# Activation halves as one 512-column matmul, and second products by pairs of output tiles, in a two-block transformer kernel

## The chip, the cores and the metric

The kernel runs on one core of a Trainium2 chip. The metric is the device time of one execution in microseconds (us). The core's engines run in parallel and wait for one another by semaphores: TensorE (PE, with its weight loads shown apart as PEld), VectorE (DVE), ScalarE (ACT), GpSimd (POOL), and SyncE (SP), which issues most transfers.

## What is computed

Two transformer blocks in float32 on one sequence of 256 rows and 1024 channels. The first block has two layers; the second has one, with a modulation by a condition vector c:

```python
for i in range(2):                                   # first block, F = 2816
    x = x + 0.5 * swiglu_ffn(rms_norm(x, ffn1_norm[i]), ffn1_w_in[i], ffn1_w_out[i])
    h = rms_norm(x, mix_norm[i])
    x = x + (pool_mixer(h, ...) if i == 0 else nsa_mixer(h, ...))
    x = x + memory_cross_attention(rms_norm(x, xattn_norm[i]), rms_norm(mem, mem_norm[i]), ...)
    x = x + 0.5 * swiglu_ffn(rms_norm(x, ffn2_norm[i]), ffn2_w_in[i], ffn2_w_out[i])
x = rms_norm(x, final_norm)
# second block: shift, scale, gate = parts of silu(c) @ ada_w + ada_b
u = rmsnorm(x, norm_mix) * (1 + scale1) + shift1
...                                                  # u @ w_in: three attentions, and gates
x = x + gate1 * ((gates[0] * y_a + gates[1] * y_b + gates[2] * y_c) @ w_o)
u2 = rmsnorm(x, norm_mlp) * (1 + scale2) + shift2
x = x + gate2 * (jnp.square(jax.nn.relu(u2 @ w_ff1)) @ w_ff2)     # 4096 hidden
return rmsnorm(x, norm_final)

def swiglu_ffn(h, w_in, w_out):
    g, u = jnp.split(h @ w_in, 2, axis=-1)
    return (jax.nn.silu(g) * u) @ w_out
```

## The kernel before

Activations live transposed: channels on the 128 partitions, the 256 rows on the free axis, eight tiles of channels. Every float32 operand is split exactly into two float32r parts, hi and lo. A product of a 128x128 weight tile with 256 columns is three float32r matmuls of 256 columns that add up in PSUM (`mm3`, L154 to L159): w_hi with x_hi (L157), w_hi with x_lo (L158), w_lo with x_hi (L159). Each loads its own weights. Where the result has rows on partitions (`row_tiles`), the activations are the loaded side and 256 columns of a weight slab move.

Weights come in slabs of 1 MB, [128, 2048] a partition, by transfers that SP issues into four `raw` buffers. Each slab is split in halves of 1024 elements: ACT casts the hi part (`hi`, L98), DVE subtracts it from the raw weights for the lo part (`lo`, L104), into six buffers for each part.

A swiglu feed-forward (`_swiglu`) runs over 11 slabs j, each of two hidden tiles. One slab takes two `w_in` slabs (gate and up halves) and one `w_out` slab. `product` makes 32 products for the two hidden tiles, gate and up beside each other in one PSUM bank for each tile. `evacuate` (L397 to L407) multiplies a bank by the rows' norm factor (DVE, 128x512, L399), takes the silu (ACT, L401), the product of the halves (DVE, L403), and splits the result (ACT L98, DVE L104). `output(j - 2)` makes the 16 second products of a slab two slabs later; they add up in four PSUM banks `acc`, which are held through the whole feed-forward. `residual` (L463 to L471) adds the result to x at the end, by eight DVE instructions of 128x256.

Other work is traced between the slabs. `middle[j]` is a step of it at slab j. The `modulation` steps (L1025 to L1030) are DVE work on slabs of ada_w, on 9 of 11 slabs in the second feed-forward of layer 0 and in the first of layer 1, and on 6 in the last one. `fill` traces steps of a generator that waits for gaps; `mem_kv`, the memory's keys and values for the cross-attention, is one with 8 slabs a layer, and `fill(after)` places some of its steps at the ends of phases. In `_xattn` each head's products with `w_o` are part of that head's stage of the pipeline (L697 to L704). `merge` and `_mlp` are built like the feed-forward, with slabs of w_o, of w_ff1 and w_ff2.

The order on each engine is the order in which the program is traced, as far as the tile scheduler leaves it; it moves instructions of different phases past each other where their operands allow it. PSUM has eight banks of [128, 512] float32: four in the pool `pm` (products on their way out), and four that a phase takes for its own.

## Time and profile before

| what | value |
|---|---|
| runs | 1582.41, 1581.73 us and one of 6651.41; median 1582.41 us |
| the profiled execution's own span | 1590.3 us |
| PE busy | 1558.1 us, 12979 matmuls |
| DVE busy | 1120.5 us |
| ACT busy | 831.0 us |
| POOL busy | 115.4 us |
| read from HBM | 289.42 MB, 183 GB/s over the span |

The profile is of one execution, seen by the hardware's profiler. It gives each engine's busy time, and for each idle stretch what ended it. Busy shares are means over stages of different kinds: a share of a stage says more than one of the span. PE's matmuls overlap in the pipeline, so the duration shown of one matmul is longer than the distance between the starts of two; distances, or a count over a stretch without gaps, give the rate. The granted clock is PE's, as a share of its full one.

### The profile page before, as it was taken

Reading aid. Unit: us, or ns where it says so; the run is one execution under the profiler, and the core shown is the slowest. Engines: PE = TensorE matmul, PEld = TensorE weight load, DVE = VectorE, ACT = ScalarE, POOL = GpSimd, SP = SyncE. Lnnn points to the kernel's source line nnn. Section 1 sums busy time; section 2 is a strip of 40 time slices with the busy share of each in tenths; the row PEclk is TensorE's granted clock in tenths of the full one; section 3 lists DMA queues with packets and bytes.
Section 4 is the critical chain, followed back from the end, with each engine's and each line's share of the span. In section 5 each row is a group of like instructions: output and inputs, shape, how many; then the busy total and the mean of one; then the engine's idle time right before and its main releaser. Section 6 shows DMA issues by size and latency. Waiting matters only on the chain.

```text
span 1590.3 us, 31387 instructions
## 1 busy us (share of the span) xinstructions
PE 1558.1 (98%) x12979; PEld 1523.9 (96%) x12979; DVE 1120.5 (70%) x2034; ACT 831.0 (52%) x1401; POOL 115.4 (7%) x195
## 2 busy tenths in 40 slices
PE   8999999999999999999999998999999999999998
PEld 8999999999999999999986997999999999999998
DVE  6676589688787688885677666887587755885553
ACT  6544457554445444453467554444453786464443
POOL 3010022030001100011000213000000000000000
PEclk9999999999999999999999999999999999999999
DMA  8645655457776677766741335686644644545540
GB/s 267 232 167 177 206 172 168 132 182 248 248 246 214 214 241 248 254 212 195 212 107 54 132 108 164 212 266 226 202 140 127 189 138 155 184 159 188 186 160 27
DMA packets 232364, 292.52 MB, mean 184 GB/s; under 512 B 7805, under 2 KB 210460, under 8 KB 232220
## 3 DMA queue, kind: packets, MB, share of 16 engines
q1 hardware_dynamic: 231756, 289.84, 56.2%
q8 instruction: 102, 1.67, 0.4%
q10 hardware_dynamic: 464, 0.66, 0.1%
q14 instruction: 42, 0.34, 0.1%
HBM read 289.42 MB, written 1.07 MB: 183 GB/s over the span
## 4 chain that ended last, share of the span: by engine, by line
PE 89%; DVE 4%; ACT 3%; POOL 2%; issue 1%; DMA 1%; DVEq 0%; ACTq 0%; POOLq 0%
PE ps L157 28%; PE ps L158 27%; PE ps L159 27%; DVE wl L104 1%; ACT wh L98 1%; PE tr L1392 1%; PE ps L874 1%; PE o L935 1%; PE ps L483 1%; ACT pn L957 0%; DVE isc L1477 0%; DVE iwk L1485 0%; DMA dl<-in_diff_lambda_dram 0%; POOL s L339 0%; PE ps L358 0%
## 5 line engine op out<-in xcount | busy, mean ns | idle before, releaser
L98 ACT CAST wh<-raw 128x1024 fp32r<-128x1024 f32 (+1 forms) x500 | 506.7, 1028 | 569.3 <-PE ps L158 459.2
L104 DVE TENSOR_TENSOR wl<-raw,wh 128x1024 fp32r<-128x1024 f32 (+1 forms) x500 | 605.9, 1225 | 256.9 <-ACT wh L98 256.1
L157 PE MATMUL ps<-xsh,wh 128*128 128x256 f32 (+1 forms) x1928 | 546.5, 283 | 0.9 <-ACT wh L98 0.9
L159 PE MATMUL ps<-xsh,wl 128*128 128x256 f32 (+1 forms) x1928 | 543.6, 282 | 0.7 <-DVE wl L104 0.7
L158 PE MATMUL ps<-xsl,wh 128*128 128x256 f32 (+1 forms) x1928 | 543.1, 282 | 0.0
L157 PEld LDWEIGHTS ps<-xsh,wh 128*128 128x128 f32 x1928 | 364.9, 189 | 2.1 <-ACT wh L98 1.2
L159 PEld LDWEIGHTS ps<-xsh,wl 128*128 128x128 f32 x1928 | 364.8, 189 | 1.1 <-DVE wl L104 1.1
L158 PEld LDWEIGHTS ps<-xsl,wh 128*128 128x128 f32 x1928 | 364.7, 189 | 0.0
L159 PE MATMUL ps<-hh,wl 128*128 128x256 f32 x704 | 197.4, 280 | 0.0
L157 PE MATMUL ps<-hh,wh 128*128 128x256 f32 x704 | 197.3, 280 | 0.0
L158 PE MATMUL ps<-hl,wh 128*128 128x256 f32 x704 | 196.8, 280 | 0.0
L158 PEld LDWEIGHTS ps<-hl,wh 128*128 128x128 f32 x704 | 132.8, 189 | 0.0
L159 PEld LDWEIGHTS ps<-hh,wl 128*128 128x128 f32 x704 | 132.2, 188 | 0.0
L157 PEld LDWEIGHTS ps<-hh,wh 128*128 128x128 f32 x704 | 131.9, 187 | 0.2
L157 PE MATMUL ps<-xs2h,wh 128*128 128x256 f32 x320 | 92.4, 289 | 0.0
L158 PE MATMUL ps<-xs2l,wh 128*128 128x256 f32 x320 | 90.9, 284 | 0.0
L159 PE MATMUL ps<-xs2h,wl 128*128 128x256 f32 x320 | 90.8, 284 | 0.0
L1027 DVE SCALAR_TENSOR_TENSOR moda<-raw,cs,moda 128x256 f32<-128x256 f32 x168 | 81.2, 483 | 4.5
L399 DVE TENSOR_TENSOR gu<-ps,rb 128x512 f32<-128x512 f32 x88 | 58.7, 687 | 29.0 <-PE ps L159 26.1
L158 PE MATMUL ps<-h2l,wh 128*128 128x256 f32 x256 | 72.1, 282 | 0.1
L157 PE MATMUL ps<-h2h,wh 128*128 128x256 f32 x256 | 72.2, 284 | 0.0
L159 PE MATMUL ps<-h2h,wl 128*128 128x256 f32 x256 | 72.1, 282 | 0.0
(420 smaller groups left out, 2629.0 us busy)
## 6 DMA issues: line engine op xcount, KB each, us to landing
raw<-in_ffn_w_in_dram SPq DMA_DIRECT2D x86, 1024.0 KB, 6.4
raw<-in_ffn_w_out_dram SPq DMA_DIRECT2D x44, 1024.0 KB, 7.2
raw<-in_w_ff_dram SPq DMA_DIRECT2D x32, 1024.0 KB, 5.3
raw<-in_ada_w_dram SPq DMA_DIRECT2D x24, 1024.0 KB, 6.9
raw<-in_w_in_dram SPq DMA_DIRECT2D x24, 1024.0 KB, 5.2
raw<-in_xattn_w_kv_dram SPq DMA_DIRECT2D x16, 1024.0 KB, 7.4
raw<-in_nsa_w_in_dram SPq DMA_DIRECT2D x10, 1024.0 KB, 5.6
raw<-in_xattn_w_q_dram SPq DMA_DIRECT2D x8, 1024.0 KB, 5.1
```

What stands on the lines that cost most here:

```text
L98: return self.nc.scalar.copy(out, x)
L104: return self.nc.vector.tensor_tensor(out, x, h, ALU.subtract)
L157: mm(out, w[0], x[0], start=start, stop=False, skip_group_check=skip)
L158: mm(out, w[0], x[1], start=False, stop=False, skip_group_check=skip)
L159: mm(out, w[1], x[0], start=False, stop=stop, skip_group_check=skip)
L399: nc.vector.tensor_tensor(gu, ps.rearrange("p (h s) -> p h s", h=2), rb2, ALU.mult)
L483: nc.tensor.matmul(ps[:, r * n:(r + 1) * n], sq[:, r * P:(r + 1) * P], cols[:, k], start=(k == r == 0), stop=(k == KT - 1), skip_group_che ...
L874: nc.tensor.matmul(ps[:, m * 64:m * 64 + 60], w1s[j // 8][:, j % 8, m * P:(m + 1) * P], blk[:, j], start=(j == 0), stop=(j == 15))
L935: nc.tensor.matmul(o[half * 64:half * 64 + 64, (r % 2) * S + kt * P:(r % 2 + 1) * S], vS[:, i, kt, g * 64:(g + 1) * 64], pT[:, :S] if kt = ...
L1027: nc.vector.scalar_tensor_tensor(acc, raw[:, k], cs[:, k:k + 1], acc, ALU.mult, ALU.add)
L1392: nc.tensor.transpose(ps[:, j * P:(j + 1) * P], p[:, j * P:(j + 1) * P], self.ident)
```

## The change

A new product, `mm2`, has two matmuls: one of 512 columns, w_hi with [x_hi | x_lo] side by side, into a whole PSUM bank, and one of 256 columns, w_lo with x_hi, into the first half of it. The two halves of the bank are added on the way out by `added`: ACT copies the second halves, DVE adds the first ones. PSUM is now handed out in tiles of two banks (`two_banks`: two from `pm`, one from `px` within a phase, and two single banks `small`). The hi and lo parts of activations and of weights lie in one tile each.

In the feed-forward, `hidden` multiplies by the norm's factor on POOL, in SBUF, after the addition. The second products no longer follow slab by slab into banks that are held: every six hidden tiles (6, 6, 6 and 4) `down` makes them by pairs of output tiles, p = (0, 1), then 2, then 3, with slabs of up to eight rows of `w_out` by 256 columns, and adds the result to x. In the last feed-forward it runs once, behind all 22 hidden tiles (`parts=(22,)`). Cross-attention, merge and MLP make their output products by `down` as well: the cross-attention's behind its heads, the MLP's in two groups, of 12 and 20 hidden tiles. Slabs of six rows are split as 4 + 2.

`row_tiles` moves 512 columns of a `wide_slab`. `mem_kv` has 6 steps for its slabs where it had 8; of the calls of `fill(after)`, that of the pool mixer stays, and the memory's keys and values of layer 1 come within NSA's attention. The MLP's relu and square are one DVE instruction on what `added` gives, where they were one of ACT and one of DVE. The QK and PV products, the pool mixer, the index part and the merge's branches keep `mm3`. The core of the diff:

```diff
+    def mm2(self, bank, w, x, start, stop):
+        mm = self.nc.tensor.matmul
+        mm(bank.rearrange("p (t s) -> p t s", t=2), w[:, 0], x, start=start, stop=False, skip_group_check=True)
+        mm(bank[:, :S], w[:, 1], x[:, 0], start=False, stop=stop, skip_group_check=True)
+
+    def added(self, dst, pp, scale=None, n=P):
+        b = self.tmp([P, 2, S], tag="bh")
+        if scale is None:
+            self.nc.scalar.copy(b[:n], pp[:n, :, S:])
+            return self.nc.vector.tensor_tensor(dst, pp[:n, :, :S], b[:n], ALU.add)
...
     def split_slabs(self, raws, perm=(None, None), turn=1):
         rows = raws[0].shape[1]
-        n = max(1, rows // 2)
+        n = min(rows, 1024 // raws[0].shape[2])
...
-        def evacuate(ps):
-            gu = self.tmp([P, 2, S], tag="gu")
-            nc.vector.tensor_tensor(gu, ps.rearrange("p (h s) -> p h s", h=2), rb2, ALU.mult)
-            sg = self.tmp([P, S], tag="sg")
-            nc.scalar.activation(sg, gu[:, 0], AF.Silu)
-            h = self.tmp([P, S], tag="h")
-            nc.vector.tensor_tensor(h, sg, gu[:, 1], ALU.mult)
...
-        def output(j, hs):
-            wo = self.slab(wout[:, j * 2:j * 2 + 2, :], (2, D))
...
+        def hidden(f, gu):
+            nc.gpsimd.tensor_tensor(gu, gu, rb2, ALU.mult)
+            h = self.tmp([P, S], tag="sg")
+            nc.scalar.activation(h, gu[:, 0], AF.Silu)
+            nc.vector.tensor_tensor(h, h, gu[:, 1], ALU.mult)
+            hs[f] = self.tmp([P, 2, S], F32R, tag="hs", bufs=max(parts))
+            self.hi(hs[f][:, 0], h)
+            self.lo(hs[f][:, 1], h, hs[f][:, 0])
...
+            product(pp, ws, t, range(4, KT))
...
+            gu = self.tmp([P, 2, S], tag="gu", bufs=4)
+            self.added(gu, pp)
+            pend.append((f, gu))
+            while rb2 is not None and pend:
+                hidden(*pend.pop(0))
+            fs.append(f)
+            if len(fs) == parts[0] and f < F1 // P - 1:
+                self.down(wout, fs, hs, put)
+                fs = []
...
+    def down(self, w, ks, xs, put):
+        slabs = [ks[i:i + KT] for i in range(0, len(ks), KT)]
+        def part(pp, p, rows):
+            ws = self.slab(w[:, rows[0]:rows[-1] + 1, p * S:(p + 1) * S], (len(rows), S))
+            for i, k in enumerate(rows):
+                for m in range(2):
+                    self.mm2(pp[:, m], ws.tile(i, m), xs[k], start=(k == ks[0]), stop=(k == ks[-1]))
+        for ps in ((0, 1), (2,), (3,)):
+            pps = [self.two_banks() for _ in ps]
+            for rows in slabs:
+                for p, pp in zip(ps, pps):
+                    part(pp, p, rows)
+            for p, pp in zip(ps, pps):
+                put(pp, p)
+
+    def residual(self, pp, p, scale=None):
+        x = self.xT[:, 2 * p:2 * p + 2]
+        for c in (slice(0, S), slice(S, 2 * S)):
+            src = pp[:, :, c]
+            if scale is None:
+                nc.vector.tensor_tensor(x, src, x, ALU.add)
+            elif isinstance(scale, float):
+                nc.vector.scalar_tensor_tensor(x, src, scale, x, ALU.mult, ALU.add)
...
-            yield
-            wo = self.slab(wo_src[:, 2 * h:2 * h + 2, :], (2, D))
...
+        self.down(wo, list(range(KT)), [q[:, :, k] for k in range(KT)], self.residual)
...
-            ffn(0, "ffn1", middle={j: self.fill for j in range(2, 7)}, after=2, first=first)
+            ffn(0, "ffn1", middle={j: self.fill for j in range(2, 7)}, first=first)
...
-            ps = ffn(1, "ffn2", middle={2: self.lam, **{j: step for j in middle}}, cols=self.mix_columns)
+            ps = ffn(1, "ffn2", middle={2: self.lam, **{j: step for j in middle}}, cols=self.mix_columns, parts=(22,))
```

## Rows read from the trace of the kernel before

**Rows 1.** The page, part 1: busy time of each engine (share), instructions.
```profile
PE 1558.1 (98%) x12979; PEld 1523.9 (96%) x12979; DVE 1120.5 (70%) x2034; ACT 831.0 (52%) x1401; POOL 115.4 (7%) x195
```

**Rows 2.** The page, part 4: the chain that ended last, its share by engine.
```profile
PE 89%; DVE 4%; ACT 3%; POOL 2%; issue 1%; DMA 1%; DVEq 0%; ACTq 0%; POOLq 0%
```

**Rows 3.** Windows by stage: stretch, us, engines' busy us, clock, DMA share, GB/s.
```profile
319.20:507.90 188.70, 188.70 (x1594) 188.70 (x1593) 151.80 (x240) 89.99 (x131) 12.88 (x17) 1.00 0.71 235
...
713.70:899.20 185.50, 182.87 (x1493) 163.42 (x1492) 119.53 (x362) 99.90 (x238) 6.18 (x16) 1.00 0.47 137
899.20:961.20 62.00, 59.94 (x502) 59.11 (x501) 43.42 (x69) 36.30 (x67) 13.11 (x19) 1.00 0.41 135
961.20:1160.50 199.30, 191.74 (x1598) 190.06 (x1597) 146.42 (x232) 90.42 (x136) 15.14 (x17) 0.98 0.65 212
```

**Rows 4.** The waits of PE: us in total, times, longest.
```profile
PE ps L358 <- POOL rn L317: 7.5, 1, 7.5
```

**Rows 5.** Windows: busy time in 100 us without a gap on PE.
```profile
400.00:500.00 100.00, 100.00 (x846) 100.00 (x845) 80.30 (x125) 44.93 (x61) 0.00 (x0) 1.00 0.75 252
```

**Rows 6.** Windows: busy time in slabs of 17 us; the sum is over five.
```profile
428.00:445.00 17.00, 17.00 (x146) 17.00 (x145) 13.91 (x23) 7.49 (x11) 0.00 (x0) 1.00 0.75 248
...
sum 85.00, PE 85.00 PEld 85.00 DVE 69.61 ACT 37.61 POOL 0.00; mean PE 17.00 PEld 17.00 DVE 13.92 ACT 7.52 POOL 0.00
```

**Rows 7.** Windows: busy time near the start.
```profile
12.10:15.40 3.30, 3.30 (x15) 3.30 (x16) 2.48 (x5) 3.30 (x8) 0.00 (x0) 0.50 1.09 348
```

**Rows 8.** PE's timeline near the start: start, us, instruction.
```profile
12.88 0.41 PE L158 MATMUL ps<-xsl,wh 128*128 128x256 f32 x1
...
15.23 0.39 PE L157 MATMUL ps<-xsh,wh 128*128 128x256 f32 x1
```

**Rows 9.** PE's timeline at the gates' product, first and last of 23 matmuls.
```profile
769.41 0.28 PE L158 MATMUL ps<-xsl,wh 128*48 128x256 f32 x1
...
772.00 0.28 PE L159 MATMUL ps<-xsh,wl 128*48 128x256 f32 x1
```

**Rows 10.** The chain that ended last: start, us, engine, output, line.
```profile
743.38 7.09 PE ps L874 x64
```

**Rows 11.** Lines by form: busy us, mean ns | idle before, what ended it.
```profile
L399 DVE TENSOR_TENSOR gu<-ps,rb 128x512 f32<-128x512 f32 x88 | 58.7, 687 | 29.0 <-PE ps L159 26.1 <-ACT rb L365 2.4
L401 ACT ACTIVATE sg<-gu 128x256 f32<-128x256 f32 x88 | 34.4, 412 | 28.0 <-DVE gu L399 27.9
L403 DVE TENSOR_TENSOR h<-sg,gu 128x256 f32<-128x256 f32 x88 | 33.8, 419 | 1.3 <-ACT sg L401 1.3
L98 ACT CAST hh<-h 128x256 fp32r<-128x256 f32 x88 | 33.1, 406 | 13.4 <-DVE h L403 12.2
L104 DVE TENSOR_TENSOR hl<-h,hh 128x256 fp32r<-128x256 f32 x88 | 33.8, 420 | 0.4 <-ACT hh L98 0.4
L587 ACT COPY kT<-ps 128x512 f32<-128x512 f32 x8 | 4.6, 577 | 0.0
L471 DVE SCALAR_TENSOR_TENSOR xT<-ps,xT 128x256 f32<-128x256 f32 x32 | 12.0, 418 | 3.3 <-PE ps L159 3.3
```

**Rows 12.** DVE's timeline where POOL does nothing.
```profile
349.49 2.35 DVE L104 TENSOR_TENSOR wl<-raw,wh 128x1024 fp32r<-128x1024 f32 x2
...
354.58 1.28 DVE L399 TENSOR_TENSOR gu<-ps,rb 128x512 f32<-128x512 f32 x2
```

**Rows 13.** DVE's timeline beside POOL's work.
```profile
208.65 5.83 DVE L104 TENSOR_TENSOR wl<-raw,wh 128x1024 fp32r<-128x1024 f32 x3
```

**Rows 14.** POOL's timeline in the same stretch.
```profile
206.78 4.94 POOL L339 TENSOR_TENSOR s<-s,sq 128x512 f32<-128x512 f32 x3 [1.65 <-ACT sq L337]
211.79 1.60 POOL L340 TENSOR_TENSOR sqs<-s 128x256 f32<-128x256 f32 x1
```

**Rows 15.** All of POOL's additions of squares, L339: shortest/median/longest ns.
```profile
L339 POOL TENSOR_TENSOR s<-s,sq x21: 1284/1589/2262, 17.2 to 967.7; 128x512 f32<-128x512 f32 x21
```

More of the change, by code (lines that the diff above doesn't have):

```diff
@@ L132, in split_slabs @@
         rows = raws[0].shape[1]
-        n = max(1, rows // 2)
-        parts = [[self.halves(raw[:, i:i + n], *perm) for raw in raws] for i in range(0, rows, n)[::turn]]
+        n = min(rows, 1024 // raws[0].shape[2])
+        parts = [[self.halves(raw[:, i:min(i + n, rows)], *perm) for raw in raws] for i in range(0, rows, n)[::turn]]
         return [Slab(n, p) for p in zip(*parts[::turn])]
@@ L374, in rstd, with swiglu @@
         return self.all_rstd(rn, ps), rn
-    def swiglu(self, w_in, w_out, gain, middle={}, after=0, first=None, cols=None):
-        with self.phase("ffn", 4) as pa:
-            return self._swiglu(pa, w_in, w_out, gain, middle, after, first, cols)
-    def _swiglu(self, pa, w_in, w_out, gain, middle, after, first, cols):
+    def swiglu(self, w_in, w_out, gain, middle={}, after=0, first=None, cols=None, parts=(6, 16)):
+        with self.phase("ffn", True):
+            return self._swiglu(w_in, w_out, gain, middle, after, first, cols, parts)
@@ L382, in _swiglu, with product @@
+    def _swiglu(self, w_in, w_out, gain, middle, after, first, cols, parts):
         nc = self.nc
         xs = None if first else self.split(self.xT, gain)
-        acc = [self.psum(pa) for _ in range(4)]
         win = w_in.rearrange("(k p) c -> p k c", p=P)
         wout = w_out.rearrange("(k p) c -> p k c", p=P)
-        nj = F1 // S
         rb2 = None
-        def product(pss, ws, ks):
+        pend, hs = [], {}
+        def product(pp, ws, t, ks):
             for k in ks:
-                for t, ps in enumerate(pss):
-                    for hf in range(2):
-                        self.mm3(ps[:, hf * S:(hf + 1) * S], ws[hf].tile(k, t), [x[:, k] for x in xs],
-                                 start=(k == hf == 0), stop=(k == KT - 1))
@@ L445, in _swiglu @@
-        output(nj - 2, prev.pop(0))
-        if nj in middle:
-            middle[nj]()
+                for hf in range(2):
+                    self.mm2(pp[:, hf], ws[hf].tile(k, t), xs[:, :, k], start=(k == 0), stop=(k == KT - 1))
+        def hidden(f, gu):
[6 more added lines that the diff above has]
+            self.lo(hs[f][:, 1], h, hs[f][:, 0])
@@ new lines, in _swiglu, with put @@
+        tail = None
+        def put(pp, p):
+            if tail:
+                tail(p, pp)
+            else:
+                self.residual(pp, p, 0.5)
+        fs = []
+        for f in range(F1 // P):
+            j, t = f // 2, f % 2
+            if t == 0:
+                if j in middle:
+                    middle[j]()
+                if first and j == 0:
+                    xs, ws = first
+                else:
+                    ws = self.split_slabs([self.raw(win[:, :, c + j * S:c + (j + 1) * S], (KT, S)) for c in (0, F1)])
+            pp = self.two_banks()
+            if f == 0:
+                sq = self.squares(self.xT, lambda i: self.tmp([P, 2, S], tag="gu", bufs=4))
+            product(pp, ws, t, range(4))
+            if f == 3:
+                rb2 = self.all_rstd(rn, rps)[:, None, :].broadcast_to([P, 2, S])
+            product(pp, ws, t, range(4, KT))
+            if f == 1:
+                rps = self.psum()
+                rn = self.row_rstd(sq, D, rps)
+            gu = self.tmp([P, 2, S], tag="gu", bufs=4)
[6 more added lines that the diff above has]
+                self.down(wout, fs, hs, put)
+                fs = []
@@ L615, in _xattn @@
+    def _xattn(self, l):
         nc, a = self.nc, self.a
@@ L1318, in merge @@
         rows = (slice(0, 4), slice(4, 6), slice(6, KT))
[L1319 removed]
+        ms = self.pair(self.a2, KT, "xs2")
         def branches(c):
             cs = slice(c * S, (c + 1) * S)
[L1323 removed]
+            ws = self.slab([(slice(None), v, slice(None), z[:, :, cs]) for v, z in zip(rows, srcs)], (KT, S))
             t = self.tmp([P, 3, 2, S], tag="mrg")
```

624 lines of the change are left out of this document (288 added, 336 removed).

## The prediction, made before the changed kernel was run

> **What bounds the kernel now.** I read the busy shares first. TensorE (PE) is busy for 98% of the span and its weight loads (PEld) for 96%; VectorE (DVE) follows with 70% [rows 1]. The chain that ended last agrees: 89% of it is PE [rows 2]. Shares over a whole span can hide a stage with another limit, so the table by stage came next. In the second feed-forward of layer 0 PE has no idle time and DVE is busy 151.80 of 188.70 us; in the NSA stage PE is busy 182.87 of 185.50 us but its weight loads only 163.42; the cross-attention and the last feed-forward leave PE idle for 2.06 and 7.56 us [rows 3]. 7.5 us of the latter is one wait for GpSimd (POOL), for the norm's row factors [rows 4]. So what the change is worth hangs on two prices: one of PE's instructions, and DVE's time in the feed-forwards that also carry the modulation steps.
>
> The profiled execution's span is 1590.3 us, the median of the runs 1582.4. The 7.9 us between them lie in the profiled execution as a whole; my sum is of differences in the span, and I put it on the median.
>
> **PE's price before.** In 100 us without a gap PE runs 846 matmuls [rows 5], nearly all of 256 columns: 118.2 ns each, three to a product, 354.6 ns. A slab j of a feed-forward has 32 first products (2 tiles, 2 halves, 8 k) and 16 second ones: 48 x 0.3546 = 17.0 us.
>
> **How much of it a longer matmul saves.** The trace has no float32r matmul of 512 columns, so I bound it. At the start the granted clock is 0.50 [rows 7], and there eleven matmuls of 256 columns start (15.23 - 12.88)/11 = 0.2136 us apart [rows 8]. That level is 1.2 GHz; at 2.4 GHz the columns take half, 106.8 ns for 256, if those starts hold nothing but columns. So each matmul takes 118.2 - 106.8 = 11.4 ns more than its columns at full clock. If that is a cost of each instruction, the new product is 213.6 + 11.4 + 118.2 = 343 ns and saves 11.4. Upper end: it goes by columns and the product stays at 354.6, saving nothing. Lower end: the weight load set the pace. For this speaks that 64 matmuls of only 60 columns, with full 128-column loads, took 7.09 us, 111 ns each [rows 10]; then the load hides under the long matmul and the product is 213.6 + 111 = 325, saving 30. Against it: 22 matmuls from 769.41 to 772.00 us load only 48 columns and still stand (772.00 - 769.41)/22 = 118 ns apart [rows 9]; were the load the limit, a load of 48 columns should show it. I take 11.4, by the nearer row: 256 moving columns, as here.
>
> The Trainium skill (Perfetto Trace Analysis, section Identifying the Most-Contended Engine) says that a busy matmul row is no measure of TensorE's headroom and that the busy share of weight loads is one. Before is at 96% by that measure, and by that rule a third fewer loads should free nearly all that is not streaming: the 325 ns end, and the first rival below. The 48-column rows disagree with it.
>
> **What is removed and saved on PE.** Products that become one 512-column and one 256-column matmul: 4 x 11 x 48 = 2112 in the feed-forwards, 128 each for memory keys, cross-attention queries and its outputs, 192 in NSA, 320 in the second block's input projection, 64 in the merge, 480 in the MLP: 3552. The row-wise tiles (memory values, NSA values, av) go from 192 products at 256 moving columns to 96 at 512: 288 fewer matmuls. All of it: (3552 + 288) x 0.0114 = 44 us, if nothing else binds.
>
> **What is added on DVE.** Five slabs in a row of the modulated feed-forward take 17.0 us each, with DVE busy 13.92 us of them and POOL not at all [rows 6]. The multiply by the norm on the way out (L399) [rows 11] becomes the addition of the two PSUM parts, of the same shape: no change. The new copy of the second half goes to ACT, at 577 ns a tile (L587) [rows 11]; ACT is busy 7.52 us a slab [rows 6], so it is hidden, and would cost its own length if ACT were full. The residual came once per feed-forward, 8 instructions of 418 ns (L471) [rows 11]; now it comes per group of six hidden tiles, that is per three slabs, as 8 of 128x512 from PSUM: two such (L399) took 1.28 us [rows 12], so 8 x 0.64/3 = 1.7 us a slab. DVE: 13.9 + 1.7 = 15.6. The bytes of weights per slab and their splitting stay. The runs of w_out shrink from 4 KB to 1 KB, as w_in's already are; the DMA share is 0.75 at 248 GB/s there [rows 6], and the transfers run ahead of use, so I cost them at nothing; were they late, DVE and ACT would wait for them before splitting.
>
> **POOL beside DVE.** The multiply by the norm moves to POOL: two per slab, 128x512 with both operands in SBUF. Such an operation takes 1284 to 2262 ns on POOL [rows 15]. POOL is free, so its own time costs latency only. But let x be what DVE loses to each. Two large subtractions of DVE take 2.35 us without POOL (L104) [rows 12], 1.17 each; three took 5.83 while POOL was adding [rows 13, 14], 2.3 more than 3 x 1.17, with two full POOL operations and one of half size beside them: x from 0.8 to 1.2. Bounds: 0 (never beside each other) and 2.26 (all of the longest lost). I take 1.0. DVE per modulated slab: 15.6 + 2.0 = 17.6 us, against PE's 48 x 0.343 = 16.5. DVE becomes the bound there.
>
> On this the Trainium skill (SBUF — State Buffer, section Who interferes with whom) says that VectorE and GpSimd share one pair of ports as an exclusive lock, and that nothing else contends. It speaks against this change; the stretched subtractions agree. By the whole length of each POOL operation it would be the second rival's price.
>
> **The sum.**
> - 18 modulated slabs (9 each in two feed-forwards): 17.6 - 17.0 = +0.6 each, +10.8.
> - Last feed-forward: its second products all come at the end, so its six modulated slabs have 32 products, 11.35 us of PE before. DVE there: 13.9 without the two w_out subtractions (2.35) is 11.55, plus 2.0: 13.55, +2.2 each, +13.2.
> - The other 3552 - 18 x 48 - 6 x 32 = 2496 products: -28.5. Row tiles, 288 x 0.0114: -3.3.
> - New waits. The second products of a group need its last hidden tile: copy 0.58, add 0.64, POOL 1.6, then silu, product, hi, lo at 0.41, 0.42, 0.41, 0.42 [rows 11, 15]: 4.5 us. In hand are the ten products of the five earlier tiles, 3.4 us: 1.1 late, nine times, 10. At the ends of three feed-forwards the last group has four tiles, six products in hand, 2.1 us: 2.4 late, 7 in all. Queued behind on PE is the next slab; the scheduler already moves PE work out of program order, so some is covered: +12, from 0 to 17.
> - Cross-attention's output products leave the head pipeline, where they filled gaps; PE idles only 2.06 us in that stage now [rows 3]: +2 for each layer, +1 for the end, where w_ff2 runs after everything: +5.
> - Memory keys and values of layer 1 move from phase ends into NSA's pipeline, which has 2.6 us of PE idle time [rows 3]; the 7.5 us wait [rows 4] may shorten: -5, from -10 to 0.
>
> +10.8 + 13.2 - 28.5 - 3.3 + 12 + 5 - 5 = +4: **1586 us**. With x open, 24 modulated slabs give 48x - 24, and the sum is 48x - 44.
>
> **Rivals.**
> 1. *The loads set the pace* (faster): product 325 ns. The 2496 products give -75, the row tiles (576 matmuls at 118.2 become 288 at 213.6) -6.7; the rest stays: 24 - 75 - 6.7 + 12 = -46, 1537 us. For it: loads busy 96%, the 60-column row. Against: the 48-column rows. It passes 2% where the product is below about 330 ns.
> 2. *The lock decides* (slower): mechanism of POOL and DVE in the 24 modulated slabs. x = 2.2, DVE 20 us a slab, 48 x 2.2 - 44 = +62: 1644 us. From x = 1.57 on it is slower by 2%. For it: the longest POOL operation is 2262 ns. Against: DVE also has work that was not stretched, and lost half of POOL's time where both ran.
> 3. *Nothing is saved on PE* (product stays 354.6): 24 + 12 + 5 - 5 = +36, 1618 us. For it: that 48 and 128 loaded columns take the same fits a cost by moving columns. Against: the 213.6 ns at half clock, which leaves nothing for the instruction.
>
> **Chances.** Two per cent, about what a measurement of this kernel can tell from no change, lies below 1551 and above 1614 us. Forecast 0.40: with x from 0.5 to 1.5 and the waits from 0 to 17 its own range is 1551 to 1616; 0.04 of it faster, 0.35 same, 0.01 slower. Rival 1 has 0.33 (0.31 faster, 0.02 same), rival 2 0.15 (0.01 same, 0.14 slower), rival 3 0.12, on the bound (0.04 same, 0.08 slower). Faster 0.35, same 0.42, slower 0.23. The range 1530 to 1640 leaves out the lower third of rival 1 and half of rival 2, 0.18.
>
> **What would show it.** PE's price: the first feed-forward has no modulation in it; with products of 343 ns its slab is 16.5 us against 17.0, with 325 it is 15.6. The matmuls should be 12979 - 3552 - 288 = about 9140. DVE: in modulated slabs it should be busy over 95% with PE waiting for the split weights; the large subtractions take longer than 1.17 us. If PE stays without gaps there, x is below 0.45. Waits: PE on the last hidden tile's lo at nine places, about 1 us each. I am wrong if the NSA or second-block stages, where I put almost nothing, move by more than 10 us, or if the 1 KB runs make weights late: then ACT's casts wait for the w_out transfers.

## The result, and the profile after

The changed kernel takes 1718.19 us (median of four runs, 1715.51 to 1720.42) against 1583.12 before: 1.0852 times, 95% interval 1.0834 to 1.0869. It is 135 us slower; 1586 was forecast, with 1530 to 1640 as the range. The profiled execution has a span of 1714.4 us, 124.1 more than the one of before; the accounts below are of these two.

The page of the changed kernel, part 1 (compare [rows 1]) and the chain that ended last (compare [rows 2]):

```profile
PE 1596.4 (93%) x9139; PEld 1366.0 (80%) x9139; DVE 1278.9 (75%) x2217; ACT 895.2 (52%) x1525; POOL 247.9 (14%) x289
...
PE 54%; DVE 27%; ACT 7%; DMA 5%; POOL 4%; issue 4%; POOLq 0%; ACTq 0%; SPq 0%; DVEq 0%
```

The matmuls fell to 9139 as counted, the weight loads' share from 96 to 80%, and PE is busy longer than before. PE's part of the chain fell from 89 to 54%, VectorE's rose to 27%: PE waits now, and mostly for work that passes through VectorE.

Windows by stage of the changed kernel (stretch, us, busy us of PE, PEld, DVE, ACT and POOL with instructions, granted clock, DMA share, GB/s). The stretches end where a stage's residual ends: second feed-forward of layer 0, first of layer 1, NSA, second cross-attention, last feed-forward, second block's attention and merge, MLP:

```profile
352.10:562.30 210.20, 192.49 (x1059) 165.67 (x1058) 178.72 (x264) 101.30 (x155) 43.48 (x39) 0.98 0.63 202
562.30:782.00 219.70, 200.65 (x1074) 172.43 (x1073) 186.01 (x275) 101.77 (x162) 43.02 (x40) 0.95 0.63 205
782.00:1003.30 221.30, 208.92 (x1228) 167.47 (x1227) 141.45 (x387) 113.42 (x260) 20.70 (x25) 0.95 0.44 131
1003.30:1068.10 64.80, 60.69 (x380) 54.04 (x379) 50.24 (x83) 38.53 (x71) 6.93 (x17) 1.00 0.41 130
1068.10:1272.60 204.50, 196.63 (x1112) 168.13 (x1112) 162.06 (x233) 102.66 (x160) 48.62 (x39) 0.99 0.63 203
1272.60:1519.50 246.90, 229.03 (x1422) 197.13 (x1421) 175.68 (x402) 150.67 (x272) 9.12 (x27) 0.97 0.47 146
1519.50:1704.00 184.50, 184.09 (x1089) 162.74 (x1088) 124.87 (x181) 86.53 (x114) 0.00 (x0) 1.00 0.47 149
```

The same stages, side by side, from the windows of both kernels:

| stage | before, us | after, us | PE idle before | PE idle after |
|---|---|---|---|---|
| first feed-forward of layer 0 | 205.6 | 221.9 | 6.5 | 17.5 |
| pool mixer | 54.1 | 61.8 | 0.0 | 6.8 |
| cross-attention, layer 0 | 60.5 | 68.4 | 2.0 | 7.8 |
| second feed-forward of layer 0 | 188.8 | 210.2 | 0.0 | 17.7 |
| first feed-forward of layer 1 | 200.1 | 219.7 | 0.0 | 19.1 |
| NSA | 191.0 | 221.3 | 2.6 | 12.4 |
| cross-attention, layer 1 | 62.2 | 64.8 | 2.1 | 4.1 |
| last feed-forward | 202.5 | 204.5 | 7.6 | 7.9 |
| attention and merge | 228.2 | 246.9 | 3.8 | 17.9 |
| MLP | 187.2 | 184.5 | 0.1 | 0.4 |

PE's idle time rose by 111.5 - 24.7 = 87 us. The mean granted clock fell from 0.994 to 0.972; with 0.50 as the lower level that is 96 us at half clock instead of 19. PE was busy in 83 of these 96 us and in 10 of the 19. A product takes 0.64 us there and 0.354 at full clock (below), so 45% of that busy time is lost: 37 us instead of 5. 87 + 32 = 119 of the 124 us. PE's own work gave next to nothing back.

PE's timeline in a modulated feed-forward (start, us, instruction, and in brackets the idle time before it and what ended it): a stretch at full clock, then the second products of a group of six hidden tiles.

```profile
429.84 0.39 PE L188 MATMUL pp<-xs,w 128*128 128x512 f32 x1
430.07 0.28 PE L189 MATMUL pp<-xs,w 128*128 128x256 f32 x1
430.19 0.39 PE L188 MATMUL pp<-xs,w 128*128 128x512 f32 x1
...
433.38 0.39 PE L188 MATMUL pp<-xs,w 128*128 128x512 f32 x1
...
441.03 0.28 PE L189 MATMUL pp<-xs,w 128*128 128x256 f32 x1
441.15 0.40 PE L188 MATMUL pp<-hs,w 128*128 128x512 f32 x1
...
445.51 0.50 PE L188 MATMUL pp<-hs,w 128*128 128x512 f32 x1 [1.37 <-DVE hs L126]
...
453.50 0.51 PE L188 MATMUL pp<-hs,w 128*128 128x512 f32 x1 [3.60 <-DVE hs L126]
...
455.57 0.63 PE L188 MATMUL pp<-hs,w 128*128 128x512 f32 x1
456.00 0.42 PE L189 MATMUL pp<-hs,w 128*128 128x256 f32 x1
456.21 0.63 PE L188 MATMUL pp<-hs,w 128*128 128x512 f32 x1
```

From 429.84 to 433.38 lie ten products: 354 ns each, as before. The 512-column matmul stands 0.23 us ahead of the next, the 256-column one 0.12: the time goes by columns. Over the whole traces, between matmuls at full clock without idle time, the median distances are 233 and 119 ns, 352 for a product, where three times 118 was 354 before: about 2 ns saved. Behind the second wait, from 455.57 on, a product takes 0.64 us. The window there shows the half clock:

```profile
454.60:458.00 3.40, 3.40 (x12) 2.80 (x12) 3.03 (x7) 1.99 (x2) 0.00 (x0) 0.50 0.66 212
```

What the last hidden tile of that group went through. Its last product began at 441.03 and ended at 441.31; ACT's, POOL's and DVE's timelines:

```profile
444.26 0.57 ACT L195 COPY bh<-pp 128x512 f32<-128x512 f32 x1
```
```profile
445.97 1.00 DVE L1081 SCALAR_TENSOR_TENSOR moda<-raw,cs,moda 128x256 f32<-128x256 f32 x2
446.89 1.22 DVE L126 TENSOR_TENSOR w<-raw,w 128x1024 fp32r<-128x1024 f32 x1
448.02 0.69 DVE L196 TENSOR_TENSOR gu<-pp,bh 128x512 f32<-128x512 f32 x1
448.62 0.68 DVE L126 TENSOR_TENSOR w<-raw,w 128x512 fp32r<-128x512 f32 x1
449.22 1.50 DVE L1081 SCALAR_TENSOR_TENSOR moda<-raw,cs,moda 128x256 f32<-128x256 f32 x1
450.65 1.21 DVE L126 TENSOR_TENSOR w<-raw,w 128x1024 fp32r<-128x1024 f32 x1
451.78 0.41 DVE L438 TENSOR_TENSOR sg<-sg,gu 128x256 f32<-128x256 f32 x1
452.12 0.99 DVE L1081 SCALAR_TENSOR_TENSOR moda<-raw,cs,moda 128x256 f32<-128x256 f32 x2
453.03 0.42 DVE L126 TENSOR_TENSOR hs<-sg,hs 128x256 fp32r<-128x256 f32 x1
```
```profile
448.79 1.65 POOL L435 TENSOR_TENSOR gu<-gu,rb 128x512 f32<-128x512 f32 x1 [7.59 <-DVE gu L196]
```

From 441.31 to 453.45 the chain takes 12.1 us. Its own instructions are the 4.5 us that were forecast; the other 7.6 are places in line: 2.9 behind the tile before it and weight casts on ACT, 3.2 behind weight splits and modulation on DVE before the addition, 0.9 before the product and 0.4 before the split. At 449.22 a modulation step of 0.48 us takes 1.50 while GpSimd multiplies.

The waits of PE over the whole changed kernel (us in total, times, longest):

```profile
PE pp L188 <- DVE hs L126: 42.6, 20, 3.8
PE pp L189 <- DVE w L126: 10.1, 11, 2.3
PE ps L181 <- DVE pT L126: 9.1, 4, 4.6
PE ps L397 <- POOL rn L356: 7.6, 3, 3.2
```

The wait on hidden tiles is new. The one on late weights (w), which the forecast put first, is 10 us. The one for rn is 7.6 us in three places.

Before, it was one wait of 7.5 us at the start of the last feed-forward [rows 4], and that wait is not in every execution. The traces of b4 and b6 (below) are of the kernel before with an edit outside the feed-forwards. b4 has no such wait, with a span of 1582.3 us; b6 has this one:

```profile
PE ps L358 <- POOL rn L317: 1.6, 1, 1.6
```

The last feed-forward takes 194.1 and 194.8 us there, not 202.5. So this wait and the half clock behind it are very likely the 7.9 us by which the profiled execution of before is longer than the median, and the last feed-forward grew by some 10 us, not by 2. Why the wait varies is not known.

### The profile page after: what moved, and what is told of

Its sections match the earlier page's. It is cut to its first block, busy times and chain, and to the rows that moved or that the text cites. A ratio compares the mean times of both kernels' runs of the same rounds, so it can differ in the third digit from the quotient of the medians.

```text
span 1714.4 us, 24073 instructions
## 1 busy us (share of the span) xinstructions
PE 1596.4 (93%) x9139; PEld 1366.0 (80%) x9139; DVE 1278.9 (75%) x2217; ACT 895.2 (52%) x1525; POOL 247.9 (14%) x289
## 4 chain that ended last, share of the span: by engine, by line
PE 54%; DVE 27%; ACT 7%; DMA 5%; POOL 4%; issue 4%; POOLq 0%; ACTq 0%; SPq 0%; DVEq 0%
PE pp L188 27%; PE pp L189 14%; DVE w L126 12%; DMA raw<-in_ada_w_dram 3%; DVE moda L1081 3%; POOL gu L435 2%; DVE gu L196 2%; ACT w L120 2%; PE pp L183 2%; PE pp L182 2%; PE pp L181 2%; DVE sg L438 1%; DVE hs L126 1%; PE ps L927 1%; PE ps L181 1%
## 5 line engine op out<-in xcount | busy, mean ns | idle before, releaser
L188 PE MATMUL pp<-xs,w 128*128 128x512 f32 x2336 | 838.0, 400 | 8.8 <-DVE xs L127 2.9
L126 DVE TENSOR_TENSOR w<-raw,w 128x1024 fp32r<-128x1024 f32 (+1 forms) x519 | 623.1, 1210 | 165.4 <-ACT w L120 163.7
L120 ACT CAST w<-raw 128x1024 fp32r<-128x1024 f32 (+1 forms) x519 | 511.0, 997 | 340.0 <-PE pp L189 186.1
L189 PE MATMUL pp<-xs,w 128*128 128x256 f32 x2336 | 663.0, 284 | 10.4 <-DVE w L126 10.1
L188 PEld LDWEIGHTS pp<-xs,w 128*128 128x128 f32 x2336 | 444.2, 190 | 116.1 <-DVE mx L1426 3.1
L189 PEld LDWEIGHTS pp<-xs,w 128*128 128x128 f32 x2336 | 445.4, 191 | 16.7 <-DVE w L126 15.4
L188 PE MATMUL pp<-hs,w 128*128 128x512 f32 x960 | 357.4, 411 | 43.0 <-DVE hs L126 42.6
L189 PE MATMUL pp<-hs,w 128*128 128x256 f32 x960 | 276.9, 290 | 0.0
L188 PEld LDWEIGHTS pp<-hs,w 128*128 128x128 f32 x960 | 188.4, 196 | 93.6 <-DVE hs L126 49.4
L435 POOL TENSOR_TENSOR gu<-gu,rb 128x512 f32<-128x512 f32 x88 | 139.4, 1588 | 522.2 <-DVE gu L196 495.1
L189 PEld LDWEIGHTS pp<-hs,w 128*128 128x128 f32 x960 | 188.5, 196 | 0.5
L195 ACT COPY bh<-pp 128x512 f32<-128x512 f32 x144 | 83.7, 581 | 111.7 <-PE pp L189 110.7
```

The costliest lines, as they stand in the source:

```text
L120: return self.nc.scalar.copy(out, x)
L126: return self.nc.vector.tensor_tensor(out, x, h, ALU.subtract)
L188: mm(bank.rearrange("p (t s) -> p t s", t=2), w[:, 0], x, start=start, stop=False, skip_group_check=True)
L189: mm(bank[:, :S], w[:, 1], x[:, 0], start=False, stop=stop, skip_group_check=True)
L195: self.nc.scalar.copy(b[:n], pp[:n, :, S:])
L435: nc.gpsimd.tensor_tensor(gu, gu, rb2, ALU.mult)
```

## The experiments

Kernels e1 to e11 start from the changed kernel, b1 to b7 from the kernel before. Ratios are to the kernel before.

**1. What a 512-column matmul saves.**

```diff
-        mm(bank.rearrange("p (t s) -> p t s", t=2), w[:, 0], x, start=start, ...)
+        mm(bank[:, :S], w[:, 0], x[:, 0], start=start, ...)
+        mm(bank[:, S:], w[:, 0], x[:, 1], start=False, ...)
```

> The changed kernel, with each 512-column matmul written as two of 256 columns into the same two halves of the bank, and nothing else changed. Theory A (a float32r matmul costs by its columns at full clock, 118 ns for 256 and 233 for 512, so that the new form saved some 2 ns of a product's 354): 3552 products x 2 ns = 7 us slower than the changed kernel, 1720 to 1730 us. Rival (the instruction costs 11 ns, hidden now by waits elsewhere): 3552 x 11.4 = 40 us slower, some 1755 us.

1735.28 us, 1.0940 (1.0902 to 1.0977): 17 us above the changed kernel, with a spread of 14 us between its runs. That is nearer to 7 than to 40, and its mean granted clock is lower too (0.968 against 0.972). The distances between matmuls settle the price directly: 2 ns a product, 7 us in all.

**2. The lag given back.** Each group's `down` is called two hidden tiles later.

```diff
+            if due and f == due[-1] + 2:
+                self.down(wout, due, hs, put)
+                due = []
             if len(fs) == parts[0] and f < F1 // P - 1:
-                self.down(wout, fs, hs, put)
-                fs = []
+                due, fs = fs, []
```

> The changed kernel, with each group's second products traced two hidden tiles later (the way the kernel before traced them two slabs later); the group at the end of a feed-forward stays. Theory A (the loss is TensorE waiting for a group's last hidden tile, about 5 us at each of nine groups, and 3.4 us at the half clock after each): nine times 5.0 + 1.6 = 60 us faster than the changed kernel, some 1660 us. Rival B (GpSimd's multiplies slow VectorE, and the weights come late): under 10 us faster.

1690.92 us, 1.0673 (1.0657 to 1.0689): 27 us faster, not 60 as by theory A, and more than the 10 of rival B. The waits of PE show why:

```profile
PE pp L189 <- DVE w L126: 25.5, 37, 2.3
PE pp L188 <- DVE hs L126: 9.5, 5, 2.5
```

The wait on hidden tiles fell from 42.6 to 9.5 us, and the wait on split weights rose from 10.1 to 25.5. The lag moves the wait to DVE's next product, and does not shorten DVE's queue.

**3. The multiply on VectorE.**

```diff
-            nc.gpsimd.tensor_tensor(gu, gu, rb2, ALU.mult)
+            nc.vector.tensor_tensor(gu, gu, rb2, ALU.mult)
```

> The changed kernel, with the multiply by the norm's factor on VectorE instead of GpSimd. Rival B (GpSimd holds VectorE up by 1 us or more at each of 88 multiplies): faster by 30 us or more. Theory A (the wait is the chain of the last hidden tile, in which VectorE's queue is the larger part): the multiply leaves GpSimd, 1.6 us, and joins VectorE's queue, 0.6 us and a place in line; within 15 us of the changed kernel.

1654.21 us, 1.0438 (1.0420 to 1.0455): 64 us faster, with one more instruction of 0.68 us on VectorE for each hidden tile. Theory A, which expected little of this, falls. PE's waits:

```profile
PE pp L189 <- DVE w L126: 14.0, 11, 3.3
...
PE pp L188 <- DVE hs L126: 4.2, 3, 2.2
```

**4. The second block's projections as before.**

```diff
-            self.col_tiles(pp, ws, xs)
-            self.added(dst, pp, scale)
+            col3(ps, ws)                       # three matmuls of 256 into one bank
+            nc.scalar.mul(dst, ps.rearrange("p (t s) -> p t s", t=2), ...)
```

> The changed kernel, with the second block's projections and gates by three 256-column matmuls into one bank again and evacuated by ScalarE alone, as before; the number of PSUM tiles in flight stays at two. That stage is 247 us against 228 before. Theory A (VectorE's additions and the extra hop make the attention's gaps): 10 to 19 us faster than the changed kernel, 1700 to 1708 us. Rival (two PSUM tiles in flight instead of four make them): within 5 us of the changed kernel.

1702.19 us, 1.0744 (1.0720 to 1.0767): 16 us faster, a figure that the theory gave. But between the two profiled executions, of 9 us less, the stage that was edited gained 6, 240.8 us against 246.9. That the rest comes from this edit is not shown, and experiment 6 does not repeat it.

**5. GpSimd beside, not in the chain.** The multiply on VectorE, and the same once more on GpSimd into a tile `side`.

```diff
-            nc.gpsimd.tensor_tensor(gu, gu, rb2, ALU.mult)
+            nc.vector.tensor_tensor(gu, gu, rb2, ALU.mult)
+            nc.gpsimd.tensor_tensor(side, gu, rb2, ALU.mult)
```

> The changed kernel with the multiply on VectorE, as in the third experiment (1654 us), and beside it the same multiply once more on GpSimd into a tile that nobody reads, 88 times; 15 buffers for hidden tiles instead of 16. It brings back what GpSimd does to VectorE's ports, and not its place in the chain of the hidden tile. Theory A (what cost the 64 us is the chain: GpSimd's 1.6 us and one more hop through VectorE's queue, with the waits and the half clock behind it): up to 15 us above 1654. Rival B (GpSimd holds up VectorE, and that costs the 64 us): back to 1700 us or more.

1722.81 us, 1.0871 (1.0852 to 1.0891): 69 us above experiment 3. All 64 us are back, as rival B said, so the hop alone is not the cause. But here VectorE carries both its own multiply and GpSimd's hindrance, and PE's longest sum of waits is for weights (40.9 us). Experiments 7 and 8 separate the two.

**6. Experiments 2, 3 and 4 together.**

> The changed kernel with three of the edits together: the multiply on VectorE, each group's second products two hidden tiles later, and the second block's projections and gates as before. Theory A (each removes waits of its own place): 1654 - 16 - up to 10 = 1628 to 1640 us, still slower than before by 45 us or more, since the rest (cross-attention, NSA, pool mixer) is untouched. Rival (later second products meet their weights late, as the 25 us of waits for w in the second experiment suggest, and that eats the gain): 1640 to 1655 us.

1651.86 us, 1.0409 (1.0388 to 1.0431): 2 us below experiment 3 alone. With the multiply off GpSimd, the lag and the old projections bring next to nothing to the whole. The second block's attention does gain 7 us by its old projections (238.4 us against 245.7 in experiment 3), as it gained 6 in experiment 4; NSA, which was not edited, is 4 us longer (219.4 against 215.3). That fits the rival's figure of 1640 to 1655, but not its reason: PE's waits for weights are 14.2 us, as in experiment 3 (14.0).

**7 and 8. No multiply at all; and the multiply on GpSimd into a tile that nobody reads.**

```diff
-            nc.gpsimd.tensor_tensor(gu, gu, rb2, ALU.mult)
+            nc.gpsimd.tensor_tensor(side, gu, rb2, ALU.mult)     # experiment 8; nothing in 7
```

> The changed kernel without the feed-forwards' multiply by the norm's factor (left out on every engine, so the hidden tiles are not normalised). With the next run it splits the 64 us of the third experiment into GpSimd's place in the chain and GpSimd beside VectorE. Both theories: no GpSimd in the chain, none beside VectorE, and 60 us less on VectorE than the third experiment: at or below its 1654 us, 1635 to 1654.

> The same, without the multiply in the chain, and with GpSimd doing it into a tile that nobody reads: GpSimd beside VectorE, but no hop through it and no extra work on VectorE; 15 buffers for hidden tiles. Chain theory (the hop through GpSimd costs): within 15 us of the run without it, below 1670 us. Lock theory (GpSimd holds up VectorE): at least 45 us above that run, 1690 us or more. In between, both have a part, and the difference to the changed kernel's 1718 us is the chain's.

1655.77 us, 1.0439 (1.0397 to 1.0482), and 1692.91 us, 1.0660 (1.0615 to 1.0705). So, by these two, the 62 us from 1718 to 1656 split into 37 for GpSimd running beside VectorE and 25 for the hop through it; each theory alone fails. The split holds for experiment 8's place of the multiply and not in general: the multiply beside VectorE cost 69 us in experiment 5, and VectorE's instructions lost 77 us by it in experiment 8, against some 50 in the changed kernel (below). In experiment 8 the hidden tile's product of the two halves comes right while GpSimd works. Lines by form of 7 and of 8 (busy us, mean ns):

```profile
L437 DVE TENSOR_TENSOR sg<-sg,gu 128x256 f32<-128x256 f32 x88 | 36.8, 419 | 11.8 <-ACT sg L436 11.6
```
```profile
L439 DVE TENSOR_TENSOR sg<-sg,gu 128x256 f32<-128x256 f32 x88 | 83.0, 943 | 11.6 <-ACT sg L438 11.6
```

419 ns became 943: there GpSimd stretches the very link of the chain for which PE waits. In the changed kernel, where the multiply comes ahead of the silu, this product takes 518. That experiment 7, which leaves out the 60 us of multiplies that experiment 3 has on VectorE, is no faster says that VectorE's total time is not the bound.

**9. The fillers back at the phase ends,** with the multiply on VectorE (the first feed-forward likewise, `after=2`).

```diff
-            ffn(0, "ffn2", middle=middle)
-            ffn(1, "ffn1", middle=middle)
-            self.nsa(mix(1))
+            ffn(0, "ffn2", middle=middle, after=2)
+            ffn(1, "ffn1", middle=middle, after=1)
+            self.nsa(mix(1), after=1)
```

> The changed kernel with the multiply on VectorE (1654 us) and the steps of the memory's keys and values back at the ends of the phases, as before (2, 2, 1 and 1 steps). Theory (they covered the wait from a phase's last product over residual and split to the next phase's first one): 10 to 20 us below 1654. Rival (these phase ends cost nothing, since the waits inside the phases decide): within 5 us.

1648.65 us, 1.0390 (1.0348 to 1.0431): 6 us below experiment 3, inside the spread of the two, and between what the theory and the rival gave.

**10 and 11. One PSUM part in the new order;** 11 with the fillers back too.

```diff
+        mm(bank[:, :S], w[:, 0], x[:, 1], start=False, ...)      # all three into the first half
...
-            self.added(gu, pp)
+            nc.vector.tensor_tensor(gu, pp[:, :, :S], rb2, ALU.mult)
```

> The changed kernel with one PSUM part: three 256-column matmuls add up in the first half of the bank, the way out is one instruction (ScalarE's copy, or in the feed-forwards VectorE's multiply by the norm straight from PSUM, nothing on GpSimd), the residual one pass instead of two. Groups, pairs of output tiles, fillers, banks and the wide row tiles stay. Theory (the two parts cost by their hop and by VectorE's time): PE gains nothing from them, so this is 20 to 45 us below the third experiment's 1654 us, 1610 to 1634. Rival (the new order and the two PSUM tiles in flight make the rest): within 12 us of 1654.

> The same with the steps of the memory's keys and values at the phases' ends, as before. In the ninth experiment that gave 6 us, in the kernel before 12: so 6 to 12 us below the run without, 1600 to 1628 us; what then still lies above the kernel before (two PSUM tiles in flight +10, grouping +4, cross-attention +2) should be 15 to 25 us.

1652.28 us, 1.0414 (1.0363 to 1.0465), and 1653.85 us, 1.0421 (1.0382 to 1.0461). The rival of 10 holds: the copy, the addition and the residual's second pass are all gone, and the time is that of experiment 3. The 6 to 12 us expected of 11 are not there either. But the edit does two things that go against each other. Windows of the whole span (as above), experiment 3 and experiment 10:

```profile
0.00:1655.80 1655.80, 1574.58 (x9139) 1348.34 (x9139) 1277.89 (x2305) 900.18 (x1525) 111.00 (x201) 0.98 0.55 176
```
```profile
0.00:1647.40 1647.40, 1584.74 (x12691) 1527.56 (x12691) 1145.56 (x2071) 862.94 (x1449) 109.02 (x201) 0.98 0.55 178
```

PE's idle time falls from 81 to 63 us, and its busy time rises by 10, 7 of them the 3552 x 2 ns of the form with three matmuls (experiment 1). So the two PSUM parts cost nothing in sum that can be measured here, but the waits that they make, up to 18 us, are not shown to be nothing. PE's waits in 10 are small and many: 9.3 us for hidden tiles, 7.8 for pT, 6.4 for mx in the second block's attention, 4.4 for weights.

**12 to 18. Single parts put into the kernel before.** In b1 VectorE copies the bank and GpSimd multiplies; in b5 the second products come three slabs at a time without a lag; b7 joins the two; b3 takes the fillers from the feed-forwards' ends (three run after the pool mixer, the rest in and after NSA's attention); b4 puts the w_o products behind the heads; b6 holds two of the four PSUM tiles; b2 is no part of the change, but aims at the wait of [rows 4].

```diff
-            nc.vector.tensor_tensor(gu, ps.rearrange("p (h s) -> p h s", h=2), rb2, ALU.mult)
+            nc.vector.tensor_copy(gu, ps.rearrange("p (h s) -> p h s", h=2))           # b1, b7
+            nc.gpsimd.tensor_tensor(gu, gu, rb2, ALU.mult)
...
-            if j > 1:
-                output(j - 2, prev.pop(0))
+            if j % 3 == 2:                                                             # b5, b7
+                for i in range(j - 2, j + 1):
+                    output(i, prev.pop(0))
...
-                rn = self.row_rstd(sq, D, acc[0])
+                rn = self.row_rstd(sq, D, acc[0], nc.vector)                           # b2
...
-            ffn(0, "ffn2", middle=middle, after=2)
+            ffn(0, "ffn2", middle=middle)                                              # b3
...
-            yield
-            wo = self.slab(wo_src[:, 2 * h:2 * h + 2, :], (2, D))
...
         self.pipeline([head(h) for h in range(4)], between, -1)
+        for h in range(4):
+            w_o(h)                                                                     # b4
...
+            held = [self.psum() for _ in range(2)]                                     # b6
```

> The kernel before, with one thing of the change alone: VectorE copies the bank out of PSUM and GpSimd multiplies by the norm's factor in SBUF. There the second products follow two slabs later, 34 us. Theory A (GpSimd in the chain costs only where the second products stand close behind it): within 10 us of the kernel before. Rival B (GpSimd beside VectorE costs by itself, 0.5 to 1 us at each of 88 multiplies): 20 to 50 us slower.

> The kernel before, with the reciprocal root of the feed-forwards' norm and of the latent keys' norm on VectorE instead of GpSimd; nothing else. It aims at the two waits of TensorE for GpSimd's rn (7.5 and 3.0 us) and the stretches at the half clock behind them (6.8 and 3.4 us, of which a little under half is lost). If these waits set the end: 10 to 15 us faster than the kernel before. If VectorE's queue delays the result as long: no change.

> The kernel before, with the steps of the memory's keys and values taken from the ends of the feed-forwards and run later (three after the pool mixer, the rest in and after NSA's attention). If they covered anything at the feed-forwards' ends: 5 to 15 us slower than before. If not: within 5 us.

> The kernel before, with one thing of the change alone: the cross-attention's products with w_o run behind its four heads instead of in each head's last stage. If they filled the heads' waits: the changed kernel's two cross-attention stages were 7.9 and 2.6 us longer, so 6 to 12 us slower than before. If something else made those stages longer: within 4 us.

> The kernel before, with one thing alone: the feed-forwards' second products come three slabs at a time, right behind the third slab, instead of two slabs late. The chain of the last hidden tile (multiply, silu, product, split: 2.3 us by its instructions, without GpSimd and without the addition) is covered by the 32 products of earlier tiles in hand. Theory (the lag is not needed while GpSimd is out of the chain): within 8 us of the kernel before. Rival (grouping by itself makes TensorE wait, for the chain behind VectorE's queue or for the burst of w_out slabs): 15 to 40 us slower.

> The kernel before, with two of the four PSUM tiles for products held unused through the second block's attention, so that two are in flight there, as in the changed kernel. That stage and the MLP were 11 us longer in the changed kernel, and its projections back as before gave 4 to 16 of them. If the tiles in flight make them: 6 to 12 us slower than before. If not: within 4 us.

> The two together in the kernel before: GpSimd's multiply (alone +17 us) and second products three slabs at a time. Theory (the lag of two slabs is what hid GpSimd's hop): well over the sum of the two, 50 us or more slower than before. Rival (they add up): 17 us plus what grouping alone costs, within 8 us.

| kernel | what | us | ratio to before, interval |
|---|---|---|---|
| b1 | multiply on GpSimd | 1602.49 | 1.0111 (1.0090 to 1.0133) |
| b5 | groups of three slabs, no lag | 1587.34 | 1.0023 (1.0012 to 1.0034) |
| b7 | both | 1623.59 | 1.0250 (1.0232 to 1.0268) |
| b3 | fillers taken from the ends | 1597.20 | 1.0063 (1.0035 to 1.0092) |
| b4 | w_o behind the heads | 1585.91 | 1.0014 (1.0004 to 1.0023) |
| b6 | two PSUM tiles in flight | 1593.64 | 1.0063 (1.0048 to 1.0078) |
| b2 | reciprocal root on VectorE | 1578.45 | 0.9956 (0.9941 to 0.9971) |

GpSimd costs 18 us even with two slabs of lag, between the two figures for b1, and grouping 4 without GpSimd, as its theory said; together they cost 40, which is 18 more than their sum. That is the interaction, though less than the 50 us that the theory asked for, and the rival, that they add up, fails too. b4 costs too little for its theory, b3 and b6 cost what theirs said. PE's waits of b7:

```profile
PE ps L158 <- DVE hl L104: 9.6, 9, 1.3
PE ps L157 <- ACT hh L98: 9.3, 4, 3.7
```

In b3 PE waits 7.8 us for the sums of squares at the start of the pool mixer, which takes 64.4 us instead of 54.1. In b6 it stands once for the attention's maximum, which frees a PSUM tile, and that stage takes 237.0 us instead of 228.2:

```profile
PE ps L347 <- POOL sqs L340: 8.9, 3, 7.8
```
```profile
PE ps L157 <- DVE mx L1382: 8.6, 1, 8.6
```

b2 is the fastest of all kernels here, 7 us faster than before, less than the 10 to 15 that were put down if the waits set the end. Both waits for rn are gone from PE's list; but of the larger one b4 has nothing either, so most of the gain is likely the smaller one's: the second block's attention, where it stood, takes 223.0 us, against 228.2 before and 227.7 in b4.

## Why the prediction was wrong, point by point

**PE's price** failed first. A product was put at 343 ns and takes 352 to 354; the rival that nothing is saved on PE was right on this, but its sum was 1618; the 100 us above that have other causes. The step at fault took half of the 213.6 ns at half clock as the columns' share at full clock and called the other 11.4 a cost of each instruction. At full clock 512 columns take 233 ns and 256 take 118, so one instruction instead of two saves 2 x 118 - 233 = 3 ns, not 11.4; between the two levels the time of 256 columns changes by 213.6 / 118 = 1.81, not 2. A ratio of clocks was taken for a ratio of times, though a row at full clock (118 ns for 48 loaded columns as for 128, [rows 9]) already spoke for columns. Of 3552 x 11.4 ns = 40 us, nearly the whole gain, some 7 were there, by the 2 ns of a product. The lower end, 325 ns by the loads' pace, took 213.6 ns for the 512 columns as well, and failed by the same step.

The rule of the Trainium skill (Perfetto Trace Analysis, section Identifying the Most-Contended Engine), by which the busy share of weight loads shows TensorE's headroom, did not hold here: that share fell from 96 to 80% and the product's time did not move.

**VectorE as the bound** in modulated slabs, 17.6 us each, did not happen: it is busy 178.72 of 210.20 us in the second feed-forward of layer 0, 85% and not over 95, and PE waits 10 us for weights in the whole kernel. GpSimd's hindrance x was real but smaller in the mean. Lines by form of the changed kernel and of experiment 3 (modulation; mean 567 and 480 ns):

```profile
L1081 DVE SCALAR_TENSOR_TENSOR moda<-raw,cs,moda 128x256 f32<-128x256 f32 x168 | 94.9, 567 | 2.2
```
```profile
L1081 DVE SCALAR_TENSOR_TENSOR moda<-raw,cs,moda 128x256 f32<-128x256 f32 x168 | 80.6, 480 | 1.5
```

With the same difference for the weight splits (1278 and 1243 ns, 458 of them), sg (518 and 432, 88), the modulation's first step (687 and 347, 24) and the hidden split (448 and 420, 88) it is 14.6 + 16.0 + 7.6 + 8.2 + 2.5 = 49 us, 0.56 for each multiply, where 1.0 was taken.

The Trainium skill (SBUF — State Buffer, section Who interferes with whom) has VectorE and GpSimd share a pair of ports as an exclusive lock; the 0.48 us step that took 1.50 beside GpSimd, and 419 against 943 ns in experiments 7 and 8, agree.

**The waits** were the term of the sum that was mis-sized most: 12 us forecast, against 42.6 us for hidden tiles alone and 87 us more idle time of PE in all. The chain was priced as the sum of its instructions, 4.5 us. It took 12.1, because each link goes to the end of a queue that also holds weight casts, weight splits and modulation. What it costs to take a link over to another engine is that place in line, and it was not in the sum.

**The half clock** was not in the sum at all, although [rows 7] showed it. Behind the waits of a group, as at 453.50, PE ran at 0.50 for a while: 96 us in all instead of 19, and 32 us of the loss. The longest stretch, from 836.9 to 853.9 behind a wait of 1.72 us, is in NSA; the 64 matmuls of 60 columns that lie mostly in it take 12.59 us, where they took 7.09 before [rows 10]:

```profile
835.37 12.59 PE L927 MATMUL ps<-blk,raw 128*128 128x60 f32 x64 [1.72 <-DVE blk L917]
```

**The moved parts.** Fillers away from the phase ends were put at -5, in part for a wait of 7.5 us that most executions likely do not have; alone in the kernel before they cost 10 us, in the pool mixer. Cross-attention was put at +5, and its stages grew by 7.9 and 2.6 us; but the products moved behind the heads, which the forecast blamed, cost 2 us alone. Two PSUM tiles in flight where there were four were not seen; 10 us in the second block's attention. NSA and the second block, on which the forecast placed almost nothing, moved by 30 and 19 us, so it was wrong there by its own condition. Of NSA's, some 12 us are moved work: before, 105 of the 192 matmuls for the memory's keys of layer 1 ran ahead of NSA's stretch, nearly all in the first feed-forward of layer 1; now all of them run in NSA. That feed-forward lost this work and still grew by 20 us.

**What stays open.** GpSimd's multiply explains 62 to 64 of the 135 us, and by the stages most of it in the feed-forwards: the four take 856 us in the changed kernel and 804 in experiment 3. Of the other 70, single parts put into the kernel before add up to 10 + 10 + 4 + 2 = 26. Most of the 70 lies outside the feed-forwards. Experiment 3 takes 62.2 us in the pool mixer, 68.4 and 64.8 in the cross-attentions, 215.3 in NSA and 245.7 in the second block's attention, where before took 54.1, 60.5, 62.2, 191.0 and 228.2: 60 us more. Some of it fits what single parts cost at the same place: the pool mixer's 8 us b3, and the 17.5 of the second block's attention b6 (9) with the projections of experiments 4 and 6 (6 to 7); the 12 us of moved work are in NSA. These are sums of separate runs, and no run undoes these parts together. For the 10 us of the cross-attentions and the other 12 of NSA, the edit that makes them was not found. In the cross-attention the next head's scores wait 4.57 us for the pT split:

```profile
315.02 0.58 PE L181 MATMUL ps<-k,q 128*128 128x256 f32 x1 [4.57 <-DVE pT L126]
```

That split reads a PSUM tile, and `small` has two where the pool before had four; that this is the reason was only argued, not tried.

## What to carry to other kernels

A matmul's cost per instruction is read from two shapes at the same clock, or bounded down to nothing; it is not had by scaling a time from another clock. Before a link of a dependency chain goes to another engine, add its place in that engine's queue and what it does to the neighbours' instructions; and when the work that waits for the chain is brought closer behind it, the lag that hid all this is gone. When PE is the bound and hardly idle, a new wait can be paid twice, as idle time and as the half clock after it.

## What was not expected of the hardware

A float32r matmul of 256 columns takes 213.6 ns at the lower clock level and 118 at the upper, a factor of 1.81, and 512 columns take 0.23 us at the upper. Short waits of PE have such stretches behind them: after one of 3.60 us that ended at 453.50, the granted clock was 0.50 from 454.60 to 458.00; after one of 1.37 us, at 445.51, it stayed at full. At the lower level float32 matmuls of 60 columns stood 213 ns apart (from 836.9 on), as far as those of 256, and those of 512 columns 427. GpSimd's 128x512 multiply beside a VectorE instruction of 419 ns made it 943 ns in the mean of 88 (experiment 8).
